# Keeping the sums of all batches on chip and storing them once, with VectorE beginning on the first load

## The chip, the cores and the metric

The kernel runs on one core of a Trainium2 chip. The metric is the device time of one execution in microseconds (us). Executions that are compared ran on the same chip in alternating rounds. "Span" is the length of the profiled execution inside the kernel, about 1.7 us less than the time.

## The reference

```python
def setup_inputs():
    B, H, W = 4, 4224, 4224
    return {"x": np.random.randn(B, H, W).astype(np.float32)}

def reference(x):
    B, H, W = x.shape
    ps = np.cumsum(np.cumsum(x, axis=1), axis=2)
    N = min(H, W)
    diag = np.diagonal(ps, axis1=1, axis2=2)
    return np.cumsum(diag, axis=1).astype(np.float32)
```

Four matrices of 71 MB each are read once. From each come 4224 numbers.

## The kernel before

The rows arrive as strips, cast to bf16 on the way, by loads that GpSimd issues. SyncE issues one small float32 load (`head`) at the start, and the stores. VectorE, ScalarE and TensorE add each strip up. At the end of a batch, `c12` holds its sums (11 rows of 384) and they are stored. The last rows of the last batch have their own short finish.

```python
    head = last.tile([P, 2, HC], FP32, name="head")
    nc.sync.dma_start(out=head, in_=src_a[:, :, N - HC : N])
    # ...
    prefetched = []
    for i in range(NBUF):
        t = strip_tile()
        load_rows(t, 0, i * F2 * P)          # nc.gpsimd.dma_start
        prefetched.append(t)
    # ... masks and constants, on VectorE and GpSimd ...
    row_sums(hs[:, 0:2], head)               # VectorE, at the end of the setup
    # ...
    for b in range(B):
        # ... strips ...
        c12 = smalls.tile([NG, 2, GW], FP32, name="c12")
        # ... two scans write c12[:, 1, :] ...
        nc.sync.dma_start(
            out=out[b, : j1 * GW].rearrange("(g i) -> g i", i=GW),
            in_=c12[t0:NG, 1, :],
        )
    # ...
    def pair_sum(acc, src):                  # used four times at the very end
        w = src.shape[-1] // 2
        pair = last.tile([P, 288], FP32, name=f"pair{len(pairs)}")
        pairs.append(pair)
        nc.vector.scalar_tensor_tensor(
            out=pair[:, :w], in0=src[:, :w], scalar=1.0, in1=src[:, w:],
            op0=ALU.mult, op1=ALU.add, accum_out=acc,
        )
```

## Time and profile before

| | before |
|---|---|
| time, median of the first 3 runs | 668.0 us (667.62 to 669.64) |
| profiled span | 665.6 us |
| DMA engines | busy in all 40 slices |
| busiest compute engine | VectorE, 57% of the span |
| first strip used by VectorE | 34.59 us |
| last small store issued | 663.61 us, 1.94 us ahead of the end |

The page shows one digit per fortieth of the span and engine (9 is 90% busy or more) and under it what the DMA engines moved. The chain of waits gives start, length and what was done or waited for. A row of the timeline gives start, length, engine, source line, operation and tiles, with the idle time before it in brackets and what ended it. DVE is VectorE, ACT ScalarE, PE TensorE, POOL GpSimd and SP SyncE; a q behind a name is the part of the engine that issues and waits; L258 is line 258 of that kernel. A "strip" is a load's tile of rows. A "completion packet" is a packet of 4 bytes that an engine sends when its share of a transfer is done. The lines themselves stand in the prediction.

### The profile page before, as it was taken

To read this page: it belongs to the slowest core of one execution; us is meant where nothing else is said; L and a number is where in the kernel's file an instruction comes from. 1 tells how busy PE (TensorE), PEld (TensorE's weight loads), DVE (VectorE), ACT (ScalarE), POOL (GpSimd) and SP (SyncE) were. 2 spreads that over 40 slices of the span, in tenths; PEclk is the share of its full clock that TensorE was granted. 3 is DMA by queue.
4 is the path that set the end of the run, shared out by engine and by line. 5 is a ranking of instruction groups with operands and counts; after the bars stand their busy time and mean duration, and the time that the engine had idled before them with its cause. 6 is when DMAs were issued, how large, how long until landed. Compare 5 with 4: busy or idle time off the path is not lost.

```text
span 665.6 us, 2495 instructions
## 1 busy us (share of the span) xinstructions
PE 206.6 (31%) x948; PEld 94.1 (14%) x948; DVE 380.8 (57%) x176; ACT 136.1 (20%) x219; POOL 31.3 (5%) x59
## 2 busy tenths in 40 slices
PE   0071522302117143140211723404031363350418
PEld 0030211100003021010000311201000131120103
DVE  3161828476946173756794526466589433352766
ACT  0001121406300103040630020304063002030434
POOL 7000000000000000000000000000000000001000
PEclk9995857656558585665655857657565585776758
DMA  9999999999999999999999999999999999999998
GB/s 203 219 219 219 219 219 218 218 209 210 219 220 219 218 220 219 218 216 215 209 219 219 219 216 219 219 218 216 213 213 219 219 216 216 219 218 218 215 206 162
DMA packets 7672, 143.23 MB, mean 215 GB/s; under 512 B 704, under 2 KB 1004, under 8 KB 2156
## 3 DMA queue, kind: packets, MB, share of 16 engines
q0 software_dynamic: 7296, 142.47, 99.9%
q1 hardware_dynamic: 364, 0.61, 0.3%
q8 instruction: 7, 0.11, 0.1%
q14 instruction: 5, 0.04, 0.0%
HBM read 285.47 MB, written 0.07 MB: 429 GB/s over the span
## 4 chain that ended last, share of the span: by engine, by line
DVE 54%; another core or an unknown queue 37%; DMA 5%; PE 3%; issue 1%; DVEq 0%; POOLq 0%
DVE acc L258 28%; DVE mu L351 8%; DVE strip L352 8%; DVE rowed L258 7%; DMA strip<-in_x_dram 5%; DVE c L481 1%; PE d L211 1%; PE fold L218 0%; PE d L218 0%; DVE pu L258 0%; DVE c L278 0%; DVE rows L403 0%; DVE acc L376 0%; PE fold_a L218 0%
## 5 line engine op out<-in xcount | busy, mean ns | idle before, releaser
L253 ACT ACTIVATE dump<-strip 128x416 bf16<-128x416 bf16 (+6 forms) x108 | 124.4, 1151 | 520.2 <-DMA strip<-in_x_dram 517.5
L351 DVE TENSOR_TENSOR mu<-strip,um 128x4608 bf16<-128x4608 bf16 (+1 forms) x24 | 52.4, 2184 | 260.4 <-DMA strip<-in_x_dram 260.3
L258 DVE TENSOR_REDUCE acc<-strip 128x6 f32<-128x4608 bf16 (+6 forms) x23 | 195.9, 8518 | 0.4
L218 PEld LDWEIGHTS <-sel 128*11 128x11 bf16 x643 | 66.7, 104 | 482.5 <-issue 453.6
L211 PE MATMUL d<-strip,sel 128*11 128x384 bf16 x90 | 37.3, 415 | 295.8 <-DMA strip<-in_x_dram 295.8
L218 PE MATMUL d<-strip,sel 128*11 128x384 bf16 x441 | 116.6, 408 | 0.0
L352 DVE TENSOR_TENSOR strip<-strip,mu 128x4608 bf16<-128x4608 bf16 (+1 forms) x24 | 52.4, 2183 | 1.0
L211 PE MATMUL d<-mu,sel 128*11 128x384 bf16 x43 | 16.3, 379 | 108.5 <-DVE mu L351 108.5
L258 DVE TENSOR_REDUCE rowed<-strip 128x384 f32<-128x2304 bf16 x12 | 49.0, 4082 | 0.0
L218 PE MATMUL d<-mu,sel 128*11 128x384 bf16 x200 | 46.7, 369 | 0.0
L76 POOL DMA_DIRECT2D strip<-in_x_dram x24 | 16.4, 686 | 542.7 <-DVE acc L258 292.8
L253 ACT ACTIVATION_READ_ACCUMULATOR dump<-strip 128x1 f32 x108 | 20.1, 186 | 0.0
L211 PE MATMUL d<-rowed,sel_f 128*11 128x384 f32 x24 | 11.5, 566 | 20.3 <-DVE rowed L258 20.3
L211 PEld LDWEIGHTS <-sel 128*11 128x11 bf16 x134 | 13.6, 102 | 19.3 <-issue 12.3
L211 PE MATMUL d<-ident,rows 128*11 128x128 f32 x24 | 5.2, 379 | 16.8 <-DVE rows L412 16.8
L258 DVE TENSOR_REDUCE pu<-d 11x1 f32<-11x384 f32 x4 | 2.2, 545 | 6.3 <-PE d L211 6.3
L94 DVE MEMSET um<- 128x4608 bf16 (+1 forms) x2 | 4.9, 2458 | 1.1 <-issue 1.1
L95 POOL TENSOR_SCALAR_AFFINE_SELECT um<-um 128x4608 bf16<-128x4608 bf16 (+1 forms) x2 | 5.2, 2612 | 2.6 <-DVE um L94 2.6
L211 PE MATMUL d<-halves,rows 128*11 128x64 f32 x48 | 5.3, 288 | 0.0
L211 PEld LDWEIGHTS d<-ident,rows 128*11 128x11 f32 x24 | 2.5, 118 | 18.9 <-DVE rows L412 11.7
L211 PEld LDWEIGHTS d<-rowed,sel_f 128*11 128x11 f32 x24 | 1.5, 91 | 24.9 <-DVE rowed L258 24.6
L211 PEld LDWEIGHTS d<-halves,rows 128*11 128x11 f32 x48 | 4.8, 128 | 1.4 <-issue 1.3
(102 smaller groups left out, 60.6 us busy)
## 6 DMA issues: line engine op xcount, KB each, us to landing
strip<-in_x_dram POOLq DMA_DIRECT2D x19, 6336.0 KB, 72.6
strip<-in_x_dram POOLq DMA_DIRECT2D x5, 3168.0 KB, 55.8
strip<-in_x_dram POOLq DMA_DIRECT2D x1, 1080.0 KB, 49.9
strip<-in_x_dram POOLq DMA_DIRECT2D x1, 768.0 KB, 52.9
strip<-in_x_dram POOLq DMA_DIRECT2D x3, 256.0 KB, 54.1
head<-in_x_dram SPq DMA_DIRECT2D x1, 528.0 KB, 3.8
strip<-in_x_dram POOLq DMA_DIRECT2D x1, 192.0 KB, 43.2
strip<-in_x_dram POOLq DMA_DIRECT2D x1, 64.0 KB, 28.5
```

The lines of the kernel that those rows point to most:

```text
L76: nc.gpsimd.dma_start(out=o, in_=x[b, r0 : r0 + f * P, :].rearrange("(p f) w -> p f w", f=f))
L94: nc.vector.memset(um, 1.0)
L95: nc.gpsimd.affine_select(out=um, in_=um, compare_op=ALU.is_gt, fill=0.0, base=0, pattern=[[-1, f], [1, f * P]], channel_multiplier=-f,)
L211: nc.tensor.matmul(o, lhsT=lhsT, rhs=rhs, start=start, stop=False, skip_group_check=True)
L218: te.add_instruction(mybir.InstMatmult(start_tensor_calc=False, stop_tensor_calc=False, tile_position=(0, 0), tile_size=(P, P if lhsT.shap ...
L253: nc.scalar.activation(out=dump[:, :w], in_=src, func=ACT.Copy, accum_out=acc)
L258: nc.vector.reduce_sum(out=acc, in_=src, axis=AX.X)
L351: nc.vector.tensor_mul(out=mu, in0=block, in1=um)
L352: nc.vector.tensor_sub(out=block, in0=block, in1=mu)
L481: nc.vector.tensor_tensor_scan(out=c12[:, i, :], data0=ones_row, data1=src, initial=carry[:, i : i + 1], op0=ALU.mult, op1=ALU.add,)
```

## The change

The intent is to keep small stores out of the stream of loads. The sums of the three whole batches stay in one tile and are stored together, behind the first store of the last rows. VectorE begins with the row sum of the `head` load instead of the masks. To make room in SBUF, the four pair sums at the end share one scratch tile.

```diff
+    hs = last.tile([P, 3], FP32, name="hs")
+    nc.vector.reduce_sum(out=hs[:, 0:2], in_=head, axis=AX.X)
 
     sel = consts.tile([P, 2 * NG - 1], BF16, name="sel")
 ...
-        pair = last.tile([P, 288], FP32, name=f"pair{len(pairs)}")
-        pairs.append(pair)
+        if not pairs:
+            pairs.append(last.tile([P, 288], FP32, name="pair"))
+        pair = pairs[0]
 ...
-    row_sums(hs[:, 0:2], head)
 ...
+    whole_sums = last.tile([NG, LB, GW], FP32, name="whole_sums")
+    last_sums = last.tile([NG, GW], FP32, name="last_sums")
 ...
-        c12 = smalls.tile([NG, 2, GW], FP32, name="c12")
+        c1 = mup.tile([NG, GW], FP32, name="c1")
+        c2 = whole_sums[:, b, :] if whole else last_sums
 ...
-        nc.sync.dma_start(
-            out=out[b, : j1 * GW].rearrange("(g i) -> g i", i=GW),
-            in_=c12[t0:NG, 1, :],
-        )
 ...
             out=out[b, T0 : T0 + M0].unsqueeze(0), in_=yl[:, :M0]
         )
+        nc.sync.dma_start(
+            out=out[:LB, :].rearrange("b (g i) -> g b i", i=GW), in_=whole_sums
+        )
+        nc.sync.dma_start(
+            out=out[b, :T0].rearrange("(g i) -> g i", i=GW), in_=last_sums[1:NG]
+        )
```

More of the change, by code (lines that the diff above doesn't have):

```diff
@@ L303 @@
     dtot = last.tile([P, 1], FP32, name="dtot")
-    hs = last.tile([P, 3], FP32, name="hs")
     hu = last.tile([P, 3], FP32, name="hu")
     hmu = last.tile([P, 3, GW], BF16, name="hmu")
-    row_sums(hs[:, 0:2], head)
     for h in range(2):
@@ L469 @@
         pu = smalls.tile([NG, 2], FP32, name="pu")
-        c12 = smalls.tile([NG, 2, GW], FP32, name="c12")
+        c1 = mup.tile([NG, GW], FP32, name="c1")
+        c2 = whole_sums[:, b, :] if whole else last_sums
         row_sums(pu[:, 0:1], d)
-        masked(c12[:, 1, :], d, to_end, pu[:, 1:2])
+        masked(c2, d, to_end, pu[:, 1:2])
         earlier, apart = order_whole if whole else order_last
@@ L479 @@
         nc.vector.tensor_copy(out=carry, in_=carry_ps)
-        for i, src in enumerate((d, c12[:, 0, :])):
+        for i, (to, src) in enumerate(((c1, d), (c2, c1))):
             nc.vector.tensor_tensor_scan(
-                out=c12[:, i, :],
+                out=to,
                 data0=ones_row,
@@ L488 @@
             )
-        j1 = NG - t0
-        nc.sync.dma_start(
-            out=out[b, : j1 * GW].rearrange("(g i) -> g i", i=GW),
-            in_=c12[t0:NG, 1, :],
-        )
         if whole:
@@ L522 @@
         weigh_b(dtot, weights, start=True)
-        weigh_b(ones_col[0:1], c12[0:1, 1, M0:])
+        weigh_b(ones_col[0:1], last_sums[0:1, M0:])
         row_sums(asum[:, :, 1], fold_a)
@@ L541 @@
             weigh_b(bsum[:, 0, i : i + 1], weights4, R)
-        nc.vector.tensor_add(out=yl[:, :M0], in0=fin_a, in1=c12[0:1, 1, :M0])
+        nc.vector.tensor_add(out=yl[:, :M0], in0=fin_a, in1=last_sums[0:1, :M0])
         nc.sync.dma_start(
             out=out[b, T0 : T0 + M0].unsqueeze(0), in_=yl[:, :M0]
+        )
[4 more added lines that the diff above has]
+            out=out[b, :T0].rearrange("(g i) -> g i", i=GW), in_=last_sums[1:NG]
         )
```

## The prediction

> **What bounds the kernel now.** I first read the page's header with its DMA rows, then the chain of waits, then the timelines of the first 20 us and the last 6 us. The page says at once what the span is made of:
>
> ```profile
> span 665.6 us, 2495 instructions
> ...
> DMA  9999999999999999999999999999999999999998
> GB/s 203 219 219 219 219 219 218 218 209 210 219 220 219 218 220 219 218 216 215 209 219 219 219 216 219 219 218 216 213 213 219 219 216 216 219 218 218 215 206 162
> ...
> HBM read 285.47 MB, written 0.07 MB: 429 GB/s over the span
> ```
>
> The 16 DMA engines are busy in all 40 slices; no compute engine is above 57% (VectorE). The input is read as float32 and lands as bf16, so 219 GB/s into SBUF are 438 GB/s of reading. Only the first slice (203) and the last (162) are clearly below the plateau. The chain of waits agrees: VectorE works on a strip, then all wait for the next one.
>
> ```profile
> 104.54 9.06 DVE acc L258
> 113.60 11.54 another core or an unknown queue
> 125.24 2.57 DVE mu L351
> ```
>
> The 11.54 us is a wait for a load ("DMA strip<-in_x_dram" in the groups), and such pieces are 37% of the chain. Every strip has one, so VectorE and SBUF have slack of 7 to 20 us per strip. The time is: start of the first strip packet, plus the loads back to back, plus the tail behind the last load. A change can only move one of these three.
>
> **What the Trainium skill says.** (1) "DMA: Bandwidth & Descriptors", section "Where 436 GB/s comes from", puts the ceiling of the 16 ports at 435 GB/s; the trace's 429 over the whole span says nothing is left in the plateau. (2) The same page, "Queues, rings and completion order": a DMA engine takes turns between its queues, a whole packet at a time. The trace agrees: each of the 11 packets of the store at 196 us (1536 B, 0.078 us) has its 4-byte completion packet 1.94 us later on a queue of its own, which is one strip packet (25344 B, 1.886 us) in between. So a store costs its own packets and does not halt the engine until its write is confirmed. (3) "SBUF — State Buffer", section "Who interferes with whom": VectorE in a two-port mode and GpSimd writing descriptors exclude each other, and a reduction never contends. In the trace GpSimd's first load issue starts at 1.33 us, just behind the end of VectorE's small cast at 1.31 us; that fits, but does not show it.
>
> **The change part by part.**
>
> *Mid-run stores.* Before, each whole batch sends 11 rows of 1536 B while strips stream:
>
> ```profile
> out_dram<-c SPq DMA_DIRECT2D x3, 16.5 KB
> ```
>
> From the packet records: each occupies 11 of the 16 engines for 0.078 us of data plus 0.022 us of completion packet, 0.10 us per engine. I checked it against the strip packets (one per 1.867 us and engine): averaged over 16 engines, their schedule slips 0.07 us across the second store (11/16 of 0.10). Three stores: 0.30 us on each of 11 engines. A load ends with its slowest engine, so the gain is 0.30 us if that one is among the 11 and nothing if it is among the other five. At the end the engines differ by about 1.4 us. Among the packets of the fourth store, two go out at 662.25 and 662.31, next to the last strip packets of all (662.31), although this store was issued at 659.91 and its first packets left at 660.99. So late engines do carry stores. I take 0.2 to 0.3 us.
>
> *Fourth store.* It moves behind the first store of the last rows. That takes 0.087 us off 10 engines while the last pieces are loading. Some of this reaches the end: I take 0.05 us.
>
> *The late stores.* SyncE now issues two more stores after 662.01 (issue 0.23 us): one of 33 rows, one of 10. A store issue took 0.29 us in the median (0.37 at most), so SyncE is free by about 662.9, and the next store waits for ScalarE until 663.14:
>
> ```profile
> 662.01 0.23 SPq L543 DMA_DIRECT2D out_dram<-yl  x1
> ...
> 663.14 0.23 SPq L556 DMA_DIRECT2D out_dram<-yl  x1
> 663.41 0.18 DVE L561 TENSOR_TENSOR ye<-fin_e,yl 1x32 f32<-1x32 f32 x1 [0.41 <-PE fin_e L211]
> 663.61 0.23 SPq L562 DMA_DIRECT2D out_dram<-ye  x1
> ```
>
> Slack 0.2 us. Their packets, at most four per engine, take 0.31 us of a then idle engine and leave 0.7 us after issue (as the other late stores do), so they are out by about 664.0, ahead of the packet of the last store at 664.3. No cost, unless the issue of 33 rows takes twice as long as that of 11.
>
> *VectorE's order.* The sum over the first load (1.22 us) moves from 17.54 us to the front. VectorE works in order and must wait until that load has landed, 3.8 us after its issue at 0.81, so at 4.6. All its setup starts some 3.8 us later, the masks and constants end at about 22 to 23 us instead of 19.8, and the first strip is only used at 34.59 us. No cost: 11 us of slack.
>
> ```profile
> 1.33 2.26 POOL L76 DMA_DIRECT2D strip<-in_x_dram  x3 [0.81 <-POOLq L577]
> 2.21 3.90 DVE L94 MEMSET um<- 128x4608 bf16 x1 [0.90 <-issue]
> ...
> 34.59 2.56 DVE L351 TENSOR_TENSOR mu<-strip,um 128x4608 bf16<-128x4608 bf16 x1 [14.81 <-DMA strip<-in_x_dram]
> ```
>
> What can be won is the start of the strips: with VectorE silent until 4.6, GpSimd might issue at 0.9 rather than 1.33. The first strip packet went out at 3.74 us. But the first load fills the engines until about 4.0: 256 packets of 0.086 us are 1.38 us per engine, spread over 2.1 us from 1.89 on. So at most 0.7 us of engine time is idle there and 0.4 us is the most that an earlier issue gives. I take 0.15 us.
>
> *Waits.* Comparing the two programs' instructions, VectorE has the same operations. A wait on the old store before the buffer is reused goes (batches 3 and 4; the stores had landed 300 us earlier, so 0). The shared scratch tile makes the last three pair sums wait for VectorE's own previous write. Elsewhere such a wait costs 0.03 to 0.05 us of gap; two are on the closing chain (662.35 and 662.69 start at or under the end of their predecessor): +0.1 us, up to the last add at 663.41.
>
> *Sum:* -0.25 -0.05 -0.15 +0.1 = about -0.35 us, or 0.05%.
>
> **The rivals.** *Stores that stall the stream.* If the switch between reading and writing HBM cost more than the packets themselves, removing three stores would win more. For it: the third store sits in a slip of 0.27 us. Against: 0.22 us of that is the 256-byte-row transfer of diag_b, which stays, and the other two show 0.07 and about 0.1. It would be 1 us at most: 667.0. *Late stores take over the end.* If their 43 rows go out slowly, or the last small store queues behind them, the tail grows by up to 1.5 us, so 669. For it: everything behind 662.7 is serial, and the end comes 1.3 us behind the last packet. Against: the slack worked out above. *The gain is hidden anyway.* If the slowest engine is one of the five without stores (the program's own instruction fetches, 0.95 us each, hit one engine at a time), the loads gain nothing and only the 0.1 us of new waits stays: 668.1. *A bound by VectorE through the later setup* would need 11 us of delay; nothing speaks for it.
>
> **Range and chances.** I start from the median of 668.0 and take 0.4 off: 667.6. The three runs of before lie 2.0 us apart (667.62 to 669.64), far more than the effect, so the range is mostly this scatter: 666.4 to 669.0. To be over 2% faster, 13 us must go, more than start and tail hold above the streaming time; to be slower, a load would have to wait on a buffer. Faster 0.5%, same 99%, slower 0.5%.
>
> **What would show it.** DMA still 9 in every slice and 429 to 430 GB/s read. No small packets of the store queue at 196, 361 and 525 us, and the strips behind them landing about 0.1, 0.2, 0.3 us earlier relative to the first. GpSimd's first issue before 1.33 us if VectorE held it up, and at 1.33 if not. The row sum starting at about 4.6 us. The second and third of the last pair sums starting 0.03 to 0.05 us behind their predecessors. The last store issued within 0.5 us of 663.6, with SyncE free before 663.14. The prediction is wrong if a strip's multiplication starts over 1 us later or earlier, or if the time between the last small store's issue and the end (2.0 us now) grows.

## The result and the profile after

The changed kernel took 667.64 us in the median of 6 runs (667.3 to 668.98); the kernel before took 667.74 us in 6 runs (667.42 to 669.64). The ratio is 0.9999, with a 95% interval of 0.9984 to 1.0015. A ratio here is the mean time of one kernel's fast runs over that of the other's of the same rounds, so it is not quite the ratio of the medians.

The changed kernel's page, the same rows:

```profile
span 665.9 us, 2495 instructions
...
DMA  9999999999999999999999999999999999999998
GB/s 203 219 219 218 219 213 213 212 218 219 219 219 218 218 220 216 218 215 212 218 219 218 218 218 219 218 216 217 215 215 218 218 216 216 218 219 218 213 210 163
...
HBM read 285.47 MB, written 0.07 MB: 429 GB/s over the span
```

Nothing has moved: the same plateau, the same low first and last slice. The stores are gone from the stream, though. This is the DMA view of 358 to 366 us, first of the kernel before, then of the changed one (q0 carries the strips, q1 what SyncE issues):

```profile
q0 software_dynamic: 81, 1.65, 96.0%
q1 hardware_dynamic: 22, 0.02, 0.9%
```

```profile
q0 software_dynamic: 83, 1.70, 99.0%
```

The 22 packets are 11 of data and 11 of completion. The start of the changed kernel, from its timeline:

```profile
1.33 2.27 POOL L76 DMA_DIRECT2D strip<-in_x_dram  x3 [0.81 <-POOLq L584]
4.59 1.25 DVE L88 TENSOR_REDUCE hs<-head 128x2 f32<-128x1056 f32 x1 [4.59 <-DMA head<-in_x_dram]
...
23.46 0.06 DVE L377 MEMSET acc<- 128x6 f32 x1
35.16 2.56 DVE L356 TENSOR_TENSOR mu<-strip,um 128x4608 bf16<-128x4608 bf16 x1 [11.63 <-DMA strip<-in_x_dram]
```

VectorE waits for `head` until 4.59 us, as it had to, but GpSimd's first issue stays at 1.33 us. The first strip is used 0.57 us later than before: VectorE waited 11.63 us for it, and one engine's first packet had taken 3.11 us instead of about 1.9. The end, from VectorE's and SyncE's timelines:

```profile
661.72 0.41 DVE L543 TENSOR_TENSOR yl<-fin_a,last_sums 1x256 f32<-1x256 f32 x1 [0.56 <-PE fin_a L214]
...
662.64 0.39 DVE L271 SCALAR_TENSOR_TENSOR pair<-strip 128x224 f32<-128x224 bf16 x1
...
663.07 0.29 DVE L271 SCALAR_TENSOR_TENSOR pair<-strip 128x128 f32<-128x128 bf16 x1
...
663.75 0.18 DVE L568 TENSOR_TENSOR ye<-fin_e,yl 1x32 f32<-1x32 f32 x1 [0.38 <-PE fin_e L214]
```

```profile
662.52 0.31 SPq L547 DMA_DIRECT2D out_dram<-whole_sums  x1
662.87 0.34 SPq L550 DMA_DIRECT2D out_dram<-last_sums  x1
663.36 0.24 SPq L563 DMA_DIRECT2D out_dram<-yl  x1
663.96 0.23 SPq L569 DMA_DIRECT2D out_dram<-ye  x1
```

From the first to the last of these VectorE rows it is 2.03 us; before it was 1.84 (661.57 to 663.41). From the issue of the last store to the end it is 1.94 us, as before. Three questions are left. Did the stores give what was computed? Where did the tail lose 0.2 us? And what are the runs near 669 us that both kernels show?

### The profile page after: what moved, and what is told of

It reads as the page before. It is cut to its first block, busy times and chain, and to the rows that moved or that the text cites. A ratio compares the mean times of both kernels' runs of the same rounds, so it can differ in the third digit from the quotient of the medians.

```text
span 665.9 us, 2495 instructions
## 1 busy us (share of the span) xinstructions
PE 205.2 (31%) x948; PEld 94.0 (14%) x948; DVE 380.9 (57%) x176; ACT 136.1 (20%) x219; POOL 31.3 (5%) x59
## 4 chain that ended last, share of the span: by engine, by line
DVE 51%; another core or an unknown queue 35%; DMA 12%; PE 1%; issue 1%; POOL 0%; DVEq 0%; POOLq 0%
DVE acc L261 27%; DMA strip<-in_x_dram 12%; DVE mu L356 7%; DVE strip L357 7%; DVE rowed L261 7%; PE d L214 1%; DVE c L487 0%; DVE whole_sums L487 0%; POOL strip L452 0%; DVE pu L261 0%; DVE whole_sums L282 0%; POOL strip L441 0%; DVE acc L381 0%; DVE rows L408 0%
## 5 line engine op out<-in xcount | busy, mean ns | idle before, releaser
L76 POOL DMA_DIRECT2D strip<-in_x_dram x24 | 16.5, 687 | 537.9 <-DVE acc L261 292.7
```

The lines of the kernel that those rows point to most:

```text
L76: nc.gpsimd.dma_start(out=o, in_=x[b, r0 : r0 + f * P, :].rearrange("(p f) w -> p f w", f=f))
```

## The experiments

"Slip" below is worked out from the packet records. An engine sends a strip packet (25344 B) every 1.867 us. The slip is how far the mean start of 16 successive packets falls behind that schedule.

### 1. Each mid-run store sent 17 times

```diff
-        nc.sync.dma_start(
+        for _ in range(17 if whole else 1):
+            nc.sync.dma_start(
 ...
```

> The kernel before with each of its three mid-run stores sent 17 times (same data, same place): 48 stores more. Theory (a store costs its packets, 0.078 + 0.022 us on each of 11 engines): the loads end 3.4 to 4.8 us later (4.8 less the spread of 1.4 us between engines at most), ratio 1.005 to 1.007. Rival 'a store halts its engine until confirmed' (1.9 us each): 48 x 1.9 = 91 us, ratio 1.13. Rival 'hidden': 1.000.

Measured: ratio 1.0071 (1.0056 to 1.0086), median 672.7 us against 667.58. That is 4.7 us by the ratio and 5.1 us by the medians for 48 more stores, or 0.10 to 0.11 us each. Between 190 and 647 us the slip grew from 0.61 to 4.32 us, before from 0.32 to 1.56: some 0.05 us per store in the mean of 16 engines, and 0.05 x 16/11 = 0.075 on each of 11. (The very last group of 16 packets shows more, but it no longer holds all engines: followed from packet to packet, as far as the records allow it, the five engines without stores started their last strip packet by 646.5 us, the other eleven from 649.0 to 651.5.) The queue of what SyncE issues, in this run (packets, MB, share of the time of 16 engines):

```profile
q1 hardware_dynamic: 1420, 1.42, 0.8%
```

So 48 stores cost about their own packets, whose records sum to 0.10 us per store and engine, and reach the end. A store does not halt an engine until its write is confirmed (that would have been 91 us). Why the slips show 0.075 and the times 0.10 to 0.11 stays open. Whether three stores reach the end too is not settled by this: 48 make the eleven engines the last ones in any case.

### 2. Only the stores

The sums are kept and stored late, the row sum of `head` is back in its old place, and each pair sum has a scratch tile of its own, just as wide as it needs (with the old width of 288 the tiles do not fit into SBUF).

```diff
 ... (the row sum of head, moved back)
-        if not pairs:
-            pairs.append(last.tile([P, 288], FP32, name="pair"))
-        pair = pairs[0]
+        pair = last.tile([P, w], FP32, name=f"pair{len(pairs)}")
+        pairs.append(pair)
```

> Only the stores part of the change: all sums kept and stored late, but the row sum of the first load in its old place and four scratch tiles of their own size for the pair sums. Theory: no strip slips at 196, 361 and 525 us (0.07 us mean each before), and the gaps ahead of the last two pair sums are as before (start to start 0.44 and 0.34 us, against 0.58 and 0.43 in the changed kernel), so last row add 0.15 us earlier behind the first yl add than in the changed kernel (1.84 instead of 2.03 us). Ratio 0.9996. Rival 'hidden gain': 1.0000. Rival 'stores stall the stream': 0.9985 or less.

Measured: ratio 1.0001 (0.9984 to 1.0018), median 667.57 us against 667.58. Between the packets at 359 and 365 us the slip is 0.021 us, against 0.073 before, so the three single stores are worth 0.05 us each in the mean, or about 0.08 us per engine; 0.02 of the 0.07 that the prediction used is there without a store, so that the 0.07 agreed with 11/16 of 0.10 by accident. My expectation for the end missed: from the first add to the last it was 2.24 us (661.46 to 663.70), because the second-last pair sum waited 0.40 us for its data. In time, the interval decides nothing at this size.

### 3. Only the row sum first

```diff
+    hs = last.tile([P, 3], FP32, name="hs")
+    nc.vector.reduce_sum(out=hs[:, 0:2], in_=head, axis=AX.X)
 
     sel = consts.tile([P, 2 * NG - 1], BF16, name="sel")
 ...
-    row_sums(hs[:, 0:2], head)
```

> Only the second part of the change: VectorE begins with the row sum of the first load, everything else as before. Theory from the first profile: GpSimd's first load issue stays at 1.33 us although VectorE is silent until 4.6 us, the first strip packet stays at 3.7 us, setup ends at 22 to 23.5 us, ratio 1.0000. The prediction's step: issue before 1.33 us and 0.15 us gained (0.9998). Rival 'later setup costs': first strip used later than 35.0 us and ratio over 1.0005.

Measured: ratio 1.0007 (0.9989 to 1.0025), three runs at 667.3 to 667.5 and three at 669.5 to 669.8. GpSimd's first issue is at 1.33 us again: VectorE's silence does not bring it forward. The profiled execution was one of the late three. Its first strip was used at 36.57 us. That looks like the rival "later setup costs", but VectorE stood idle 13 us ahead of it, waiting for the load:

```profile
36.57 2.56 DVE L352 TENSOR_TENSOR mu<-strip,um 128x4608 bf16<-128x4608 bf16 x1 [13.02 <-DMA strip<-in_x_dram]
```

The packet records say why. Of the 16 completion packets of the first load, 14 lie between 33.92 and 34.28 us, one at 34.94 and one at 36.25. One engine's first strip packet started at 5.37 us and took 2.9 us; the others' started from 3.69 to 4.33 and most took 1.89. Every load has 16 completion packets, one per engine, and ends with the last of them. The late engine stays behind: the last two packets of 25344 B of this run start at 647.58 and 648.97 us. The same is seen in run 1 above, whose order at the start is that of the kernel before (34.68 and then 36.50 us), so VectorE's order is not its cause. The profiled run 1 is no slower for it than the other five (672.55 us, median 672.7); whether those had a late engine too is not on record.

### 4. The changed kernel twice more

> The changed kernel unchanged, for its scatter. Theory: the change gives 0.2 us at the loads (three stores gone) and takes 0.2 us at the end (two new waits of VectorE on itself), so the ratio to before is 0.9995 to 1.0005. In its first profile the strip packets slipped by an extra 0.4 us (mean over 16 engines) between 60 and 95 us, which the kernel before did not show, and one engine's first strip packet took 3.1 us. Theory: both are scatter of the execution and are absent, or elsewhere, in this profile. Rival: they belong to the program (a later setup of GpSimd and VectorE); then they come back at the same times, and the first strip is again used at about 35.2 us, not 34.6.

> The changed kernel a third time, for its groups of times. Theory: again some runs near 667.5 and some 1.2 to 2 us above; fast group 0.1 us (0 to 0.3) under the fast group of before, slow group 0.3 to 0.7 us under the slow group of before (the late engine is among the 11 that carried the stores, so all 0.3 us count). Rival: the stores gave nothing, both groups equal to before within 0.1 us.

Measured: first 1.0001 (0.9986 to 1.0016), 667.41 to 669.07 us; then 0.9985 (0.9971 to 0.9999), all five from 667.26 to 667.52. The slip of 0.4 us between 60 and 95 us of the first profile did not come back (0.15 and 0.13 us), so it was scatter. The first strip was used at 35.08 and 34.69 us; one engine was again somewhat late in the first of the two (34.74 us, 14 others by 34.15).

The second ratio looks like a gain only because none of its five runs was a late one, while four of the eleven of before were. So I pooled all runs of both kernels and cut at 668.4 us, a gap chosen by eye:

| kernel | runs | below 668.4: number, mean | above: number, mean |
|---|---|---|---|
| before | 28 | 20, 667.60 us | 8, 669.44 us |
| changed | 17 | 12, 667.44 us | 5, 668.83 us |

In the lower group the changed kernel is 0.16 us faster by the means and 0.11 by the medians, with a standard error of about 0.07 from the scatter in the groups (0.27 and 0.13 us). With a cut that was chosen on the same numbers this is a hint of a gain and not a shown one. In the upper group the runs are too few and the lateness too varied to read a difference from.

### 5. The changed kernel with four scratch tiles

The edit of the scratch tile as in run 2, on the changed kernel.

> The changed kernel with a scratch tile of its own size for each of the four pair sums instead of one shared tile; nothing else. Theory: the last pair sum starts again under the end of the one before (0.05 us of overlap, against 0.03 us of gap in both profiles of the changed kernel), 0.08 us; the pair sum before it starts when its data lands (ScalarE starts on the same piece within 0.02 us), so its wait costs nothing. In time not to be told from the changed kernel: ratio to before 0.9993 to 1.0003. Rival (the prediction's +0.1 us on the closing chain): start of the first yl add to the last add falls from 2.03 to under 1.90 us.

Measured: ratio 0.9997 (0.998 to 1.0015), median 667.89 us against 667.88; the profiled run was a very late one (670.34 us). Its end, VectorE's timeline:

```profile
664.60 0.41 DVE L542 TENSOR_TENSOR yl<-fin_a,last_sums 1x256 f32<-1x256 f32 x1 [0.56 <-PE fin_a L214]
664.94 0.44 DVE L270 SCALAR_TENSOR_TENSOR pair<-strip 128x288 f32<-128x288 bf16 x1
...
665.31 0.38 DVE L270 SCALAR_TENSOR_TENSOR pair<-strip 128x224 f32<-128x224 bf16 x1
...
665.62 0.28 DVE L270 SCALAR_TENSOR_TENSOR pair<-strip 128x128 f32<-128x128 bf16 x1
...
666.29 0.18 DVE L567 TENSOR_TENSOR ye<-fin_e,yl 1x32 f32<-1x32 f32 x1 [0.38 <-PE fin_e L214]
```

First to last add: 1.69 us, as the rival said, not my theory. The fair comparison is with a profile of the shared tile in which the data was there in time as well. The third run of the changed kernel is one (ScalarE had the same piece at 662.38 us, VectorE took it at 662.56):

```profile
662.08 0.43 DVE L271 SCALAR_TENSOR_TENSOR pair<-strip 128x288 f32<-128x288 bf16 x1
662.45 0.07 DVE L271 DVE_READ_ACCUMULATOR pair<-strip 128x1 f32 x1
662.56 0.39 DVE L271 SCALAR_TENSOR_TENSOR pair<-strip 128x224 f32<-128x224 bf16 x1
...
662.99 0.29 DVE L271 SCALAR_TENSOR_TENSOR pair<-strip 128x128 f32<-128x128 bf16 x1
```

From one pair sum to the next: 0.48 and 0.43 us with the shared tile, 0.37 and 0.31 with own tiles. Each wait on the write before it costs about 0.11 us: a gap of 0.03 to 0.04 us, and an overlap of 0.07 us that is lost. Two of them make 0.23 us on the closing chain when the data is there; where the chain waits for data, part of it is hidden. So it is in the first profile of the changed kernel: VectorE took the piece of 224 at 662.64 us and ScalarE its half at 662.63, so the data came then and the first wait cost nothing. Of the 0.19 us that this tail lost, 0.09 is the second wait (0.43 us from one pair sum to the next, 0.34 before) and the rest is data that came later.

Own tiles win almost nothing all the same. From the first add to the end of the span it is 4.07 us in the third run of the changed kernel and 4.03 here (4.05 in run 7, also with own tiles), because the stretch behind the issue of the last store has grown from 1.94 to 2.13 us (2.15 in run 7). The reason is in SyncE's waits at the very end (who waited for what: us in total, times, longest), first of the kernel before, then of this run:

```profile
SPq L588 <- DMA out_dram<-ye: 0.3, 1, 0.3
```

```profile
SPq L594 <- DMA out_dram<-whole_sums: 0.4, 1, 0.4
```

With the last add earlier, it is the late stores that SyncE waits for: by the semaphore records the store of 10 rows lands at 667.61 us and the very last store at 667.62, and SyncE checks them one after the other. Run 3, which has own tiles, data in time and no late stores, needs 1.69 us from add to add like this run, but 3.84 us to the end. So the shared tile and the late stores each cost the tail some 0.2 us, and each hides the other.

### 6. The first load sent later

To see whether the late engine comes from the meeting of the `head` packets with the first strip packets, the kernel before got its `head` load behind the second strip and its sums behind the fourth.

```diff
-    nc.sync.dma_start(out=head, in_=src_a[:, :, N - HC : N])
 ...
-    row_sums(hs[:, 0:2], head)
-    ... (the masked sums of head)
 ...
+            if b == 0 and s == 1:
+                nc.vector.memset(head[:, 0, 0:1], 0.0)   # SyncE waits for it
+                nc.sync.dma_start(out=head, in_=src_a[:, :, N - HC : N])
+            if b == 0 and s == 3:
+                row_sums(hs[:, 0:2], head)
+                ... (the masked sums of head)
```

> The kernel before with its first load (528 KB by SyncE) sent behind the second strip's sums instead of at the start, its sums behind the fourth strip; the strips have the DMA engines to themselves at the start. Question: what makes the two groups of times (about 667.5 and 669.3) that every kernel shows; in the profiles of the slow group one DMA engine's first strip packet starts at 5.3 us instead of about 4.0, takes 2.9 to 3.2 us instead of 1.9, and every load ends 1 to 2.3 us later. Theory 'collision': that engine is held by the packets of the first load; then the 16 first strip packets here start within 0.5 us of each other near 3.7 us and all times lie within 0.6 us of one another, about 1.0 us above the fast group (1.38 us of packets per engine leave the idle start), near 668.5. Rival 'the engine is late for another reason': times again in two groups 2 us apart, about 668.5 and 670.5.

Measured: 668.5 to 668.95 us in five runs, ratio 1.0005 (0.9991 to 1.0019). The first strip packets go out from 2.85 to 3.46 us, 0.9 us earlier than with `head` ahead of them, but each takes 2.3 to 3.0 us. The first load completes on all 16 engines between 33.34 and 34.14 us. Its piece of the chain of waits, and then that of run 5, the latest one:

```profile
1.33 33.14 DMA strip<-in_x_dram
```

```profile
1.33 35.71 DMA strip<-in_x_dram
```

The first packets lie within 0.6 us, near 2.9 and not 3.7 us; the times lie within 0.5 us, as the theory "collision" said, and 1.1 us above the lower group of before, because the packets of `head` now lie in the stream: 256 packets of 0.098 us in the mean are 1.6 us per engine, and between 60 and 190 us the slip grows by 1.7 us, before by 0.2.

### 7. Both: the first load later, the sums stored late

> Both: the first load sent later as in the run before, and all sums stored late with own scratch tiles. Theory: 0.2 to 0.3 us under the run before, no second group; ratio to before about 1.000 (no slow group, but 0.8 us more in the fast one). Rival: two groups, ratio 1.001 to 1.002.

Measured: 668.47 to 669.17 us in six runs, ratio 1.0005 (0.9991 to 1.0019). Again no second group, and no gain over run 6 (668.77 against 668.75 in the medians) where 0.2 to 0.3 us were expected; the late stores took 0.2 us of it back at the end (2.15 us behind the issue of the last store, in run 6 1.94), and six and five runs with 0.2 us of scatter leave the rest open.

Of the kernels with `head` at the start, 20 of 63 runs with rounds lie above 668.4 us (run 1 not counted). If runs 6 and 7 had the same share of executions with a late engine, none in 11 would have a chance of 0.68 to the 11th, 1.5%. The late engine needs the early `head` load, as far as these runs go (runs of one set may share a cause, so 1.5% is an estimate). How that load delays one engine is not seen in any record, and stays open.

### 8. The late stores

Once the two late stores were left out (the result is then wrong), and once the store of 33 rows was sent as three.

> The changed kernel without its two late stores (so its result is wrong on purpose: only the last 384 sums are written). Theory: they cost the end nothing; from the issue of the very last store to the end of the span stays 1.9 to 2.0 us (1.99 before, 1.94 and 1.95 in the changed kernel), and the store ahead of it starts as soon as ScalarE has its data. Rival 'the late stores take over the end': that time falls by 0.3 us or more.

> The changed kernel with the late store of the three whole batches sent as three stores of 11 rows instead of one of 33: one packet count, two issues more on SyncE (0.31 us each and 0.04 us between). Theory: SyncE is then free at about 663.9 counted from a first yl store at 662.2, some 0.5 us after ScalarE has the next store's data, so that store goes 0.5 us late and the last one about 0.2 us late; the end moves by 0.2 us. Rival 'SyncE has room anyway': the last store follows the last add within 0.05 us as before.

Measured, one look each: without them the end comes 1.91 us behind the issue of the last store (1.92 to 1.94 with them), so in the changed kernel they cost the end nothing that can be told. With an earlier last store they do (run 5). Sent as three, SyncE's timeline is

```profile
661.73 1.07 SPq L548 DMA_DIRECT2D out_dram<-whole_sums  x3
...
663.22 0.25 SPq L565 DMA_DIRECT2D out_dram<-yl  x1
...
```

ScalarE had the data of the third store at 662.88 us, so this store went 0.34 us late; 0.5 had been expected. The last one, issued at 663.51, was on time: its add ended at 663.48, for in this execution the pair sum ahead of it had waited 0.45 us for data. In the changed kernel itself SyncE is free at 663.21 and needed at 663.34: the slack is 0.13 us (0.15 and 0.05 in its two other profiles).

## Why the prediction was right

The predicted time was 667.6 us; 667.64 were measured. "Same" was right. That the number fits to 0.04 us is luck: the prediction started from 668.0 us for the kernel before, which took 667.74 in the rounds of the comparison, and took 0.4 off, where the medians differ by 0.10. Of the terms of its -0.35 us not all held.

- **The bound.** Right. The plateau of loads sets the time, and the 429 GB/s did not move. But the comparison of 429 with 435 GB/s does not show it: 435 is for the ports of SBUF, into which 219 GB/s go here; 429 is what is read. What shows the bound is the DMA row, 9 in nearly every slice.
- **Mid-run stores, 0.2 to 0.3 us.** That a store costs about its packets is shown, with 0.10 to 0.11 us per store by the times of run 1. In the changed kernel itself the three single stores removed 0.05 us of mean slip each, some 0.2 us per carrying engine, at the low end. That this reached the end of the execution is not shown.
- **Fourth store, 0.05 us.** Not told apart by any run.
- **Late stores, no cost.** Right for the changed kernel; without them (section 8) the end comes no sooner. But the slack was 0.13 us, not 0.2: a store issue took 0.31 and 0.34 us here, and SyncE was free at 663.21 us and not before 663.14. Their packets took 0.17 us in the mean, not 0.078, and were out at 664.30, not 664.0. They cost nothing only because the last store came later too; with own scratch tiles they cost 0.2 us (run 5).
- **VectorE's order, no cost.** Right: the setup ended at 23.5 us, 11.6 us ahead of the first strip.
- **The earlier start, 0.15 us.** Wrong. This term was taken from a coincidence: GpSimd's issue at 1.33 us behind VectorE's cast ending at 1.31. It stays at 1.33 (1.32 in two profiles) with VectorE silent until 4.6 us. The room for it was too large as well: the 256 packets of the first load took 0.120 us in the mean, 1.9 us per engine; the 0.086 of the sum is their median.
- **The new waits, 0.1 us.** Undersized for each wait. The prediction counted only the gap and not the overlap that is lost: 0.11 us each, 0.23 us for two when the data is in time. In two of the three profiles of the changed kernel the first wait was hidden behind data, and what is left, 0.09 us, is the predicted sum by luck.
- **The sum.** -0.2 for the stores, 0 for the start and +0.09 to +0.23 for the waits leave between 0 and -0.1 us; the lower group of runs hints at -0.16, with an error of 0.07.
- **The rivals.** Stalling stores are excluded by run 1, and late stores that take over, for the changed kernel, by run 8. A gain that is wholly hidden is not excluded: the intervals of the ratios of the changed kernel and of run 2 hold 1.0000 or end within 0.0001 of it, and only the lower group hints at a gain. The prediction rightly made its range from the scatter of 2 us, without knowing where that comes from: in the profiles of runs 3 and 5, both from the upper group, it is one DMA engine that starts late.

No version ran that clearly beats both. The changed kernel with own scratch tiles (run 5) loses to the late stores what it wins at the pair sums. A version with own tiles and the whole sums stored at another time was not tried.

## What to carry to other kernels

When the DMA engines are full from start to end, a small store costs about its packets, on the engines that carry it; count them before moving a store, for three of them took 0.2 us of 668 from the engines that carried them. A scratch output that is shared to save space puts a wait between instructions that overlapped before: give it its own exact width instead. When a closing chain gets shorter, look at what ends next: here the late stores took the 0.2 us back. Before reading a difference of a few tenths of a per cent, look for groups in the single times and for what the profile of a late one has that the others have not; here it was one engine's first packet.

## What the Trainium skill lacked or had wrong

- "DMA: Bandwidth & Descriptors" says in "Latency and other measured facts" that two of the 16 engines are usually slower than the rest, but has nothing on one being late when a load from SyncE and the first loads from GpSimd start together. (The packet records here do not number the engines, so whether it is one of those two is not known.) Here, in three profiles, one engine completed the first load at 36.25 to 36.74 us and the others by 34.4 to 34.9, and 20 of 63 executions took 1 to 3 us longer; none of 11 did without the early load.
- The same page, section "Latency and other measured facts", gives a first byte about 1 us after the issue for loads from GpSimd. Here the first packet left 1.5 us behind the start of the issue with idle engines (1.33 to 2.85 us), and 2.4 us behind it with the first load ahead (to 3.7 us).
- The same page, section "Anatomy of one DMA — SWDGE (gpsimd) path", gives a fixed cost of about 2 us per DMA, and the section on bandwidth warns of transfers under 64 KB. Neither says what a small store takes from a full stream: 0.10 to 0.11 us for 16.5 KB here, by the times of run 1.
- "SBUF — State Buffer", section "Who interferes with whom", says that GpSimd's descriptor writing and VectorE in a two-port mode exclude each other. No run here shows it at the start: the issue at 1.33 us did not move with VectorE silent. That does not contradict the page; the prediction's reading of the coincidence was wrong.
- "VectorE: DVE Perf Modes", section "The DRAIN you can't avoid", says that a semaphore after each operation costs nothing extra, measured on a row of eight copies. Here a pair sum that waits for VectorE's own write starts 0.11 us later than one that does not, of which 0.07 us is lost overlap.
